# Gates of the second plain pair ahead of the first token-major group in a macaron trunk

## The chip, the cores and the metric

The kernel runs on one core of a Trainium2 chip. The metric is device time in microseconds (us) of one execution, the median of several runs. The profile is of one execution of its own.

## The reference

Two layers. Each has a feed-forward block (FFN), a mixing block of three attentions, and a second FFN, with a norm on both sides of every block. In the kernel the FFNs are named a0, c0, a1, c1, and the mixing blocks b0, b1. Only the FFN is touched by the change:

```python
def _swiglu(t, w_gate, w_up, w_down):
    return (jax.nn.silu(t @ w_gate) * (t @ w_up)) @ w_down
...
    f = _swiglu(_rmsnorm(h, ffn1_pre_g[l]), ffn1_w_gate[l], ffn1_w_up[l], ffn1_w_down[l])
    h = h + 0.5 * _rmsnorm(f, ffn1_post_g[l])
```

There are 512 tokens, a model width of 1024 and 2816 hidden features, 22 blocks of 128. All is float32.

## The kernel before

**Precision.** Every operand of a large product is split into a high part (ScalarE, L188) and a low part (VectorE, source minus high part, L189). A product is three matmuls (L214 to L216): high by high, high by low, low by high. So each unit of weights (128 x 1024 elements, 512 KB) passes through a landing buffer ("raw", 2 buffers) and then through one buffer each of "wh" and "wl" (4 of each). A unit's buffers come free when the matmuls that read it are done. The transfers are issued by SyncE (SP) in order.

**An FFN** works through its 22 feature blocks in three ways.

1. *The halved pair*, blocks 16 and 17, is computed first, one half of the tokens after the other, with features on the partitions. It holds four PSUM banks of the tag "mm" (two gates, two ups; there are four of that tag). `hidden` then forms silu(gate) x up and splits it.
2. *The token-major groups*, blocks 0 to 15 in four groups of four, are computed by a seven-product scheme over halves of tokens, columns and the inner dimension. Its products are numbered 0 to 6, and each takes 24 matmuls of 512 columns and two units of weights. Products 0, 1 and 6 read the inputs themselves (tiles us), products 2 to 5 read sums of inputs (tiles ag), which `sums` prepares in three steps on VectorE and ScalarE. Products 2, 3, 5 and 6 also form sums of weights on VectorE (L337, L340, L345, L349). The first group runs in the order 0 to 6: product 0 and product 1 open two "mm" banks each, product 3 accumulates on those of product 0, and product 2 opens another two, so that it needs those of product 1 back, which VectorE has added into the result by then (L749). The other groups run in the order 0, 2, 3, 4, 5, 1, 6. At the end of a group `feature_major` turns the result.
3. *The plain pairs*, blocks 18, 19 and 20, 21, are computed feature-major over all tokens: `gates` makes two banks of 48 matmuls in all, `ups` two more, and `hidden` combines them.

**The down projection** of blocks 0 to 15 is the same scheme with seven products for each of two halves (`downs(0)`, `downs(1)`; tiles pd, on four banks "z"). For each product VectorE also prepares the other factor (`first_factor`, L849 to L855) and adds the result (L889). The plain pairs stand between these products. Blocks 16 to 21 follow in a plain down projection.

**Order.** `ffn` puts jobs in a queue Q, each with its weight units. When a job starts, the units of the next jobs are loaded ahead, four at most (`load_ahead`), and their transfers are started as far as the landing buffers allow (`fetch_ahead`). Within that the framework orders the instructions of each engine by its own estimate. In program order the jobs around the change are: both halves of the halved pair (with step 1 of the sums in the second half), `park` (saves the residual to HBM), step 2 of the sums, product 0 of the first group, step 3, products 1 to 6, the other groups, down products 0 and 2, the gates of 18 and 19, the last group's turn, down products 3, 4, 5, the ups of 18 and 19, down products 1 and 6, then 0, 2, 3 of the second half, the gates of 20 and 21, 4, 5, 1, 6, the ups of 20 and 21. Between gates and ups the two gate banks stay occupied. Temporary tiles (`tmp`) have the tag f32t with 5 buffers.

Of the kernel before, what the change touches and what calls it, by code (L numbers as in the profile page):

```python
# [17 lines left out]
P = 128  # L18
# [4 lines left out]
def kernel(  # L23
# [39 lines left out]
    _, S, D = x.shape  # L63
# [3 lines left out]
    ND = D // P  # L67
# [32 lines left out]
    def tmp(name):  # L100
        return sb.tile([P, S], F32, tag="f32t", bufs=5, name=name)
# [6 lines left out]
    def blk(tag, name):  # L108
        return stile([P, 2, S], tag, name)

    def pbank(tag, name):
        return ps.tile([P, S], F32, tag=tag, bufs=4, name=name)
# [72 lines left out]
    def split(h_ap, l_ap, src, scale=None, later=False):  # L185

        if scale is None:
            both = [nc.scalar.copy(h_ap, src)]  # L188
            make = lambda: nc.vector.tensor_tensor(l_ap, src, h_ap.bitcast(F32), ALU.subtract)  # L189
        else:  # L190
            both = [nc.scalar.activation(h_ap, src, AF.Copy, scale=scale)]
            make = lambda: nc.vector.scalar_tensor_tensor(l_ap, src, scale, h_ap.bitcast(F32), ALU.mult, ALU.subtract)
        if later:
            return make
        both.append(make())
        if Q.pinned:
            for ins in both:
                tc.keep_in_program_order(ins)
# [13 lines left out]
    def mm3(pt, lh, ll, rh, rl, start, stop, free=False):  # L212

        nc.tensor.matmul(pt, lh, rh, start=start, stop=False, skip_group_check=free)  # L214
        nc.tensor.matmul(pt, lh, rl, start=False, stop=False, skip_group_check=free)  # L215
        nc.tensor.matmul(pt, ll, rh, start=False, stop=stop, skip_group_check=free)  # L216

    def gemm(pt, units, m, act, ks=None):

        last = sum(un.nk for un in units) - 1  # L220
        for un in units:
            for k in range(un.nk):
                kk = un.k0 + k
                if ks is not None and kk not in ks:
                    continue
                c = slice(m * P, (m + 1) * P)
                ah, al = act(kk)
                mm3(pt, un.h[:, k, c], un.l[:, k, c], ah, al, kk == 0, kk == last)
                yield 3 * pt.shape[1] * PE_US
# [138 lines left out]
    def wpair(src, ktiles, c0, name, scale=None):  # L368

        return [Unit(src, k, min(4, ktiles - k), c0, 256, f"{name}_{k}", scale) for k in range(0, ktiles, 4)]  # L370
# [110 lines left out]
    Q = Queue()  # L481
# [162 lines left out]
    def ffn(l, src, wg, wu, wd, dst, name, spare, aside=None):  # L644
# [5 lines left out]
        hid, st = {}, {}  # L650
        hr = {}
        act = lambda k, c=FULL: quad_act(src.us)(k, c)

        def hidden(f, pg, pu):
            s = tmp(f"s{name}_{f}")
            nc.scalar.activation(s[:], pg[:], AF.Silu)
            nc.vector.tensor_tensor(s[:], pu[:], s[:], ALU.mult)
            t = blk("q" if f < EARLY + 2 else "o", f"hid{name}_{f}")
            hid[f] = t[:, 0], t[:, 1]
            split(*hid[f], s[:])  # L660
            if f == NF - 1:
                tc.keep_in_program_order(nc.scalar.preload_act_table_set("natural_log_exp_and_others"))
# [124 lines left out]
        def park():  # L787

            if src.name != "x":
                for t in range(NT):  # L790
                    nc.sync.dma_start(hsave[t], hT[t][:])

        def halved(f, ug, uu, half):
            if half == 0:
                st["p"] = [pbank("mm", f"p{x}{name}_{f + m}") for x in "gu" for m in range(2)]
            else:
                Q.hold, Q.pinned = False, True
                Q.load_ahead()
                Q.pinned = False
                next(summed)  # L800
            c = HALVES[half]

            for uns, pts in ((ug, st["p"][:2]), (uu, st["p"][2:])):
                for low in (False, True):
                    for un in uns:
                        for k, (m, pt) in itertools.product(range(un.nk), enumerate(pts)):
                            kk, cols = un.k0 + k, slice(m * P, (m + 1) * P)
                            wh, wl = un.h[:, k, cols], un.l[:, k, cols]
                            ah, al = act(kk, c)
                            if low:  # L810
                                nc.tensor.matmul(pt[:, c], wh, al, start=False, stop=False, skip_group_check=True)
                                nc.tensor.matmul(pt[:, c], wl, ah, start=False, stop=kk == ND - 1, skip_group_check=True)
                            else:
                                nc.tensor.matmul(pt[:, c], wh, ah, start=kk == 0, stop=False, skip_group_check=True)
                            yield (1 + low) * S // 2 * PE_US
            if half == 1:
                for m in range(2):
                    hidden(f + m, st["p"][m], st["p"][2 + m])

        def gates(f, ug):  # L820
            st[f] = [pbank("mm", f"pg{name}_{f + m}") for m in range(2)]
            for m in range(2):
                yield from gemm(st[f][m][:], ug, m, act)

        def ups(f, uu):
            for m in range(2):
                pu = pbank("mm", f"pu{name}_{f + m}")
                yield from gemm(pu[:], uu, m, act)
                hidden(f + m, st[f][m], pu)
# [78 lines left out]
        def behind():  # L908
            for job in later:
                Q.add(*job)  # L910
            later.clear()

        def some(n):
            for one in itertools.islice(todo, n):
                Q.add(*one)

        def turns(f):
            *jobs, turn = group(f)
            later.append(turn)
            return iter(jobs)  # L920

        def downs(ci):
            Q.add([], lambda: iter(first_factor(ci, 0) or ()))
            return products(ci)

        ug, uu = (wpair(w[l], ND, EARLY * P, f"{x}{name}_{EARLY}") for x, w in (("g", wg), ("u", wu)))
# [4 lines left out]
        add_sums = lambda: Q.add([], lambda: iter(next(summed) or ()))  # L931
        Q.add(ug + uu, lambda: halved(EARLY, ug, uu, 0), src.ready((0, 1)))
        Q.add([], lambda: halved(EARLY, ug, uu, 1), src.ready(range(NT)))
        Q.add([], lambda: iter(park() or ()))
        marks["first"] = len(Q.jobs)
        add_sums()
        todo = turns(TG[0])
        some(1)
        add_sums()
        some(7)  # L940
        if name == "a0":
            Q.add([], vectors)
            Q.add([], lambda: iter(mem_stats() or ()))
        for g in TG[1:]:
# [3 lines left out]
            behind()  # L948
            some(7)
            later[:] = over  # L950
        pairs = [(wpair(wg[l], ND, f * P, f"g{name}_{f}"), wpair(wu[l], ND, f * P, f"u{name}_{f}")) for f in (18, 20)]
        todo = downs(0)
        some(2)
        Q.add(pairs[0][0], lambda: gates(18, pairs[0][0]))
        behind()
        some(3)
        Q.add(pairs[0][1], lambda: ups(18, pairs[0][1]))
        some(7)
        todo = downs(1)
        some(3)  # L960
        norm = aside() if aside is not None else None
        Q.add(pairs[1][0], lambda: gates(20, pairs[1][0]))
        some(4)
        if aside is not None:
# [753 lines left out]
    for l in LAYERS:  # L1718
        i, mn = 3 * l, []
        ma = ffn(l, subs[i], ffn1_w_gate, ffn1_w_up, ffn1_w_down, subs[i + 1], f"a{l}", "v",  # L1720
                 lambda l=l, mn=mn: mem_norm(l, mn))
        values = mem_kv(l, mn, *kvs[l])
        mb = mixing(l, subs[i + 1], *kvs[l], values, subs[i + 2])
        if l == 0:
            Q.weave(begin(), ma["first"])
            more_constants()
        else:
            for part, units in zip(mc["next"], (ma["early"][:2], ma["early"][2:])):
                part.extend(units)
            boundary(mc, mc["end"], ma["first"])  # L1730
        boundary(ma, ma["end"], mb["first"])
        mb["run"]()
        mc = ffn(l, subs[i + 2], ffn2_w_gate, ffn2_w_up, ffn2_w_down, subs[i + 3], f"c{l}", "o")
        for part, units in zip(mb["next"], (mc["early"][:2], mc["early"][2:])):
                part.extend(units)
        boundary(mb, mb["end"], mc["first"])
# [25 lines left out]
```

## Time and profile before

| | |
|---|---|
| median of 3 runs | 2427.16 us (2426.83 to 2427.58) |
| profiled execution, time | 2428.36 us |
| profiled execution, span | 2426.6 us |
| mean granted TensorE clock | 0.99 |
| TensorE busy | 2380.1 us, 98% of the span |
| VectorE busy | 1872.7 us, 77% |
| ScalarE busy | 1402.5 us, 58% |
| HBM traffic | 143 GB/s over the span |

Rows of the profile name the engine (PE, PEld, DVE, ACT, POOL, SP), the line of the kernel, and the tiles as output<-inputs with their numbers left out. A letter at the end of a tile's name is the FFN's (pta and ptc are banks of token-major products in a0 and a1, and in c0 and c1; pda and pdc are those of the down products; pga and pgc are gates). In brackets stands the time that the engine sat idle just before, and who ended it. Matmuls overlap: the step from one start to the next is the pace, and the duration is longer than that.

### The profile page before, as it was taken

How to read it: one execution, taken by the hardware profiler on the slowest of the kernel's cores; microseconds unless marked ns; L12 is line 12 of the kernel's file. 1: busy time of each engine (PE TensorE's matmuls, PEld its weight loads, DVE VectorE, ACT ScalarE, POOL GpSimd, SP SyncE). 2: the span in 40 equal slices, each digit the busy share in tenths (PEclk: the TensorE clock that was granted, in tenths of full speed). 3: DMA queues.
4: the chain of work that ended last, by engine and by line, in shares of the span. 5: the costliest groups of instructions: out<-in, count | busy, mean ns of one | idle time of the engine just before them, and what ended most of it. 6: DMA issues, size and time to landing. Idle time of an engine off the chain costs nothing.

```text
span 2426.6 us, 31086 instructions
## 1 busy us (share of the span) xinstructions
PE 2380.1 (98%) x11688; PEld 2003.4 (83%) x11688; DVE 1872.7 (77%) x2532; ACT 1402.5 (58%) x2291; POOL 74.1 (3%) x130
## 2 busy tenths in 40 slices
PE   8999999999999999999989999999999999899998
PEld 6788888888888887888878888888888888788887
DVE  8788877678777687788787888676787866788885
ACT  5656555577665554565645664556675655556654
POOL 1000000001010000000000000000001100000000
PEclk9999999999999999999999999999999999999999
DMA  5465475222223454644635555642232244455544
GB/s 174 156 209 156 156 241 159 72 80 75 82 68 121 148 165 131 216 149 154 220 129 183 179 159 175 232 131 79 62 88 79 77 132 140 138 177 179 165 165 165
DMA packets 232603, 349.73 MB, mean 144 GB/s; under 512 B 10730, under 2 KB 117506, under 8 KB 231940
## 3 DMA queue, kind: packets, MB, share of 16 engines
q1 hardware_dynamic: 232352, 347.71, 45.2%
q8 instruction: 92, 1.51, 0.3%
q14 instruction: 59, 0.48, 0.1%
q0 software_dynamic: 96, 0.03, 0.0%
q10 hardware_dynamic: 4, 0.00, 0.0%
HBM read 333.02 MB, written 14.68 MB: 143 GB/s over the span
## 4 chain that ended last, share of the span: by engine, by line
PE 81%; DVE 8%; DMA 4%; ACT 3%; issue 2%; POOL 0%; DVEq 0%; ACTq 0%; POOLq 0%
PE pg L216 3%; PE pg L214 3%; PE pg L215 3%; PE ptc L215 3%; PE ptc L216 3%; PE pta L215 3%; PE ptc L214 3%; PE pta L216 3%; PE pta L214 3%; PE pdc L214 2%; PE pdc L215 2%; PE pdc L216 2%; PE pda L215 2%; PE pda L214 2%; PE pda L216 2%
## 5 line engine op out<-in xcount | busy, mean ns | idle before, releaser
L214 PE MATMUL pg<-us_a,wh_wg 128*128 128x512 f32 x384 | 151.0, 393 | 0.0
L216 PE MATMUL pg<-us_a,wl_wg 128*128 128x512 f32 x384 | 149.7, 390 | 0.0
L215 PE MATMUL pg<-us_a,wh_wg 128*128 128x512 f32 x384 | 149.6, 390 | 0.0
L188 ACT CAST wh_ta<-kta 128x1024 fp32r<-128x1024 f32 x80 | 83.3, 1053 | 92.2 <-DVE kta L337 26.2
L188 ACT CAST wh_tc<-ktc 128x1024 fp32r<-128x1024 f32 x80 | 83.2, 1051 | 88.1 <-DVE ktc L337 24.4
L189 DVE TENSOR_TENSOR wl_tc<-ktc,wh_tc 128x1024 fp32r<-128x1024 f32 x80 | 96.8, 1222 | 35.9 <-ACT wh_tc L188 35.5
L189 DVE TENSOR_TENSOR wl_ta<-kta,wh_ta 128x1024 fp32r<-128x1024 f32 x80 | 96.9, 1222 | 33.6 <-ACT wh_ta L188 33.3
L214 PE MATMUL pta<-wh_ta,aga 128*128 128x512 f32 x256 | 102.9, 404 | 13.6 <-ACT wh_ta L188 11.7
L214 PE MATMUL ptc<-wh_tc,agc 128*128 128x512 f32 x256 | 102.4, 401 | 9.8 <-ACT wh_tc L188 9.8
L215 PE MATMUL ptc<-wl_tc,agc 128*128 128x512 f32 x256 | 102.2, 399 | 3.5 <-DVE wl_tc L189 3.5
L215 PE MATMUL pta<-wl_ta,aga 128*128 128x512 f32 x256 | 102.6, 401 | 3.0 <-DVE wl_ta L189 3.0
L216 PE MATMUL pta<-wh_ta,aga 128*128 128x512 f32 x256 | 101.9, 398 | 0.0
L216 PE MATMUL ptc<-wh_tc,agc 128*128 128x512 f32 x256 | 101.6, 397 | 0.0
L214 PE MATMUL pda<-wh_da,aha 128*128 128x512 f32 x224 | 87.3, 390 | 0.0
L214 PE MATMUL pdc<-wh_dc,ahc 128*128 128x512 f32 x224 | 87.3, 390 | 0.0
L215 PE MATMUL pda<-wl_da,aha 128*128 128x512 f32 x224 | 87.2, 389 | 0.0
L215 PE MATMUL pdc<-wl_dc,ahc 128*128 128x512 f32 x224 | 87.1, 389 | 0.0
L216 PE MATMUL pdc<-wh_dc,alc 128*128 128x512 f32 x224 | 86.8, 389 | 0.0
L216 PE MATMUL pda<-wh_da,ala 128*128 128x512 f32 x224 | 86.8, 389 | 0.0
L216 PEld LDWEIGHTS pg<-us_a,wl_wg 128*128 128x128 f32 x384 | 72.1, 188 | 15.3
L215 PEld LDWEIGHTS pg<-us_a,wh_wg 128*128 128x128 f32 x384 | 72.2, 188 | 14.1
L214 PEld LDWEIGHTS pg<-us_a,wh_wg 128*128 128x128 f32 x384 | 72.1, 188 | 14.1
(543 smaller groups left out, 7522.3 us busy)
## 6 DMA issues: line engine op xcount, KB each, us to landing
raw_ta<-in_ffn_w_gate_dram SPq DMA_DIRECT2D x64, 512.0 KB, 3.8
raw_tc<-in_ffn_w_gate_dram SPq DMA_DIRECT2D x64, 512.0 KB, 3.8
raw_da<-in_ffn_w_down_dram SPq DMA_DIRECT2D x58, 512.0 KB, 3.9
raw_dc<-in_ffn_w_down_dram SPq DMA_DIRECT2D x58, 512.0 KB, 3.5
raw_wg<-in_w_gate_dram SPq DMA_DIRECT2D x48, 512.0 KB, 3.6
kta<-in_ffn_w_up_dram SPq DMA_DIRECT2D x32, 512.0 KB, 5.6
ktc<-in_ffn_w_up_dram SPq DMA_DIRECT2D x32, 512.0 KB, 5.8
raw_wo<-in_w_out_dram SPq DMA_DIRECT2D x24, 512.0 KB, 3.4
```

What stands on the lines that cost most here:

```text
L188: both = [nc.scalar.copy(h_ap, src)]
L189: make = lambda: nc.vector.tensor_tensor(l_ap, src, h_ap.bitcast(F32), ALU.subtract)
L214: nc.tensor.matmul(pt, lh, rh, start=start, stop=False, skip_group_check=free)
L215: nc.tensor.matmul(pt, lh, rl, start=False, stop=False, skip_group_check=free)
L216: nc.tensor.matmul(pt, ll, rh, start=False, stop=stop, skip_group_check=free)
```

## The change

The gates of blocks 18 and 19 are queued behind step 2 of the sums and ahead of the first token-major group, with step 3 of the sums behind them. Each of the two gate banks is passed through silu as soon as its matmuls are done; the result stays in SBUF until the ups of 18 and 19, and the banks come free. In the down projection the gates are gone from their place behind product 2, and the ups of 18 and 19 are queued behind product 3 in place of product 5.

```diff
@@ ffn @@
-        def hidden(f, pg, pu):
+        def silu(f, pg):
             s = tmp(f"s{name}_{f}")
             nc.scalar.activation(s[:], pg[:], AF.Silu)
+            return s
+
+        def hidden(f, pg, pu):
+            s = silu(f, pg) if pg is not None else st.pop(("silu", f))
             nc.vector.tensor_tensor(s[:], pu[:], s[:], ALU.mult)
...
-        def gates(f, ug):
+        def gates(f, ug, ahead=False):
             st[f] = [pbank("mm", f"pg{name}_{f + m}") for m in range(2)]
             for m in range(2):
                 yield from gemm(st[f][m][:], ug, m, act)
+                if ahead:
+                    st["silu", f + m], st[f][m] = silu(f + m, st[f][m]), None
...
         marks["first"] = len(Q.jobs)
+        pairs = [(wpair(wg[l], ND, f * P, f"g{name}_{f}"), wpair(wu[l], ND, f * P, f"u{name}_{f}")) for f in (18, 20)]
+        add_sums()
+        Q.add(pairs[0][0], lambda: gates(18, pairs[0][0], True))
         add_sums()
         todo = turns(TG[0])
-        some(1)
-        add_sums()
-        some(7)
+        some(8)
...
-        pairs = [(wpair(wg[l], ND, f * P, f"g{name}_{f}"), wpair(wu[l], ND, f * P, f"u{name}_{f}")) for f in (18, 20)]
         todo = downs(0)
         some(2)
-        Q.add(pairs[0][0], lambda: gates(18, pairs[0][0]))
         behind()
-        some(3)
+        some(1)
         Q.add(pairs[0][1], lambda: ups(18, pairs[0][1]))
         some(7)
```

## The prediction

> **What bounds the kernel now.** I read the page first, for who is busy.
>
> ```profile
> span 2426.6 us, 31086 instructions
> ...
> PE 2380.1 (98%) x11688; PEld 2003.4 (83%) x11688; DVE 1872.7 (77%) x2532; ACT 1402.5 (58%) x2291; POOL 74.1 (3%) x130
> ```
>
> TensorE (PE) is the bound, so only its stops and its slow stretches can be won. The second view is the list of who waited for whom, PE alone, over the whole span (us in total, times, longest).
>
> ```profile
> PE pta L214 <- ACT wh_ta L188: 11.7, 2, 6.7
> PE ptc L214 <- ACT wh_tc L188: 9.8, 2, 4.9
> PE ptc L215 <- DVE wl_tc L189: 3.5, 3, 1.5
> PE pta L215 <- DVE wl_ta L189: 3.0, 2, 1.5
> ...
> PE ptc L214 <- ACT sc L656: 1.0, 2, 0.8
> ```
>
> Two waits in the a-layers and two in the c-layers: one per feed-forward block (FFN), four in all. They belong to pta/ptc, the banks of the token-major groups. The third view is PE's timeline around the one of the first c-layer (start and duration in us).
>
> ```profile
> 893.37 0.40 PE L214 MATMUL ptc<-wh_tc,us_b 128*128 128x512 f32 x1
> ...
> 905.20 0.39 PE L216 MATMUL ptc<-wh_tc,us_b 128*128 128x512 f32 x1
> 910.49 1.22 PE L214 MATMUL ptc<-wh_tc,agc 128*128 128x512 f32 x2 [4.90 <-ACT wh_tc L188]
> 913.20 0.80 PE L215 MATMUL ptc<-wl_tc,agc 128*128 128x512 f32 x1 [1.49 <-DVE wl_tc L189]
> ...
> 914.22 0.63 PE L215 MATMUL ptc<-wl_tc,agc 128*128 128x512 f32 x1
> 914.64 0.63 PE L216 MATMUL ptc<-wh_tc,agc 128*128 128x512 f32 x1
> ...
> 918.75 0.39 PE L214 MATMUL ptc<-wh_tc,agc 128*128 128x512 f32 x1
> ```
>
> Products 0 and 1 of group 0 (inputs us_b) run from 893.37 to 905.43, then the first product on the summed inputs (agc) waits. After the wait the step between starts is 0.43 us (914.22 to 914.64) until 918.75, from where a matmul lasts 0.39 again as it did before. The windows of this stretch show the clock and who works meanwhile (length, then PE, PEld, DVE, ACT, POOL busy and counts, granted PE clock, DMA share, GB/s).
>
> ```profile
> 905.43:910.49 5.06, 0.16 (x2) 0.01 (x1) 5.06 (x5) 2.99 (x4) 0.00 (x0) 0.78 0.18 68
> 910.49:918.75 8.26, 6.77 (x15) 4.86 (x16) 4.98 (x6) 1.95 (x2) 0.00 (x0) 0.51 0.00 0
> ```
>
> VectorE (DVE) is busy for all 5.06 us in which PE stands: the bound here is DVE. Its own timeline says with what.
>
> ```profile
> 893.62 1.23 DVE L189 TENSOR_TENSOR wl_tc<-raw_tc,wh_tc 128x1024 fp32r<-128x1024 f32 x1 [1.38 <-ACT wh_tc L188]
> ...
> 900.57 2.35 DVE L337 TENSOR_TENSOR ktc<-ktc,raw_tc 128x1024 f32<-128x1024 f32 x2
> 902.84 1.22 DVE L677 TENSOR_TENSOR rc<-us_b 128x1024 f32<-128x1024 f32 x1
> ...
> 911.92 2.35 DVE L189 TENSOR_TENSOR wl_tc<-ktc,wh_tc 128x1024 fp32r<-128x1024 f32 x2
> 914.19 1.28 DVE L749 TENSOR_TENSOR cc<-cc,ptc 128x512 f32<-128x512 f32 x2
> 921.47 1.23 DVE L189 TENSOR_TENSOR wl_tc<-ktc,wh_tc 128x1024 fp32r<-128x1024 f32 x1 [6.00 <-ACT wh_tc L188]
> ```
>
> From 893.62 to 915.47 DVE never rests: the end of the halved pair, input sums (L677), and the weights of products 1 (L189 at 893.62), 2 (L337 at 900.57) and 3 (L189 at 911.92). Then it rests for 6.00 us: a backlog of one moment, no lasting shortage. The end of it is what PE wants twice over. Product 3's low weights come at 911.92. And product 1 is added into its result (L749) at 914.19, before which product 2 has no PSUM: there are four "mm" banks, products 0 and 1 hold two each, and product 0's pair is kept for product 3. So PE starts on product 3 and gets no further.
>
> **What one stop costs.** In the last window PE issues 15 matmuls, 15 x 0.227 = 3.40 us at full pace. From 905.43 to 918.75 are 13.32 us, so 9.92 us are lost: 4.90 + 1.49 idle, and 3.53 in the slow clock. Over the four FFNs, with the same 3.53 for each: 11.7 + 9.8 for the first waits, 4 x 1.5 for the second, 4 x 3.53 for the clock = 41.6, and 1.0 for the bank that waits for the halved pair's silu (L656): 42.6 us, 10.65 per FFN. That is all that can be won here.
>
> On the clock the Trainium skill ("TensorE: Matmul & The Clock Gate", Part 1) says that the array falls to half its rate after an idle window of about 3.4 us and needs about 3.4 us of work to come back. The step of 0.43 us against 0.227, behind 4.90 us of idleness, agrees. By that rule a wait that stays under 3.4 us would cost its own length alone.
>
> **The change, part by part.** The gates of blocks 18 and 19 are 2 x 8 x 3 = 48 matmuls. Where they stand now, the windows show what they take, and the whole stretch from the first down product to the gates of 20 (here in the last FFN, columns as above):
>
> ```profile
> 2275.35:2286.24 10.89, 10.89 (x50) 8.96 (x49) 9.37 (x11) 5.71 (x8) 0.00 (x0) 1.00 0.32 109
> ...
> 2264.47:2337.42 72.95, 72.73 (x329) 60.24 (x328) 60.94 (x68) 42.64 (x59) 0.00 (x0) 1.00 0.53 171
> ```
>
> 10.89 / 48 = 0.227 us is the full pace used above. They cost PE 10.89 us in either place: nothing is won by them themselves.
>
> *New place.* PE runs gates from 893.4 to 904.3, product 0 to 909.7, product 1 to 915.2 (5.44 us each, 24 matmuls). Weights are loaded in the order of the queue: the gates' two units take the place that product 0's had, so they are there at 893.4; product 0's take that of product 1's, ready at about 894.9, needed at 904.3. DVE's backlog grows by the two low parts of product 1's units, 2.27 us (900.57 to 902.84 is the step of two such). It therefore reaches product 1's addition (914.19 before) at 916.5, and PE comes to it at 915.2 where it came at 905.43. What is left: 916.5 + 1.28 - 915.2 = 2.6 us, of which product 3's first unit (12 matmuls, 2.7 us) covers all if its weights are there: lower bound zero. The upper bound comes from the casts,
>
> ```profile
> L188 ACT CAST wh_tc<-ktc 128x1024 fp32r<-128x1024 f32 x80 | 83.2, 1051 | 88.1 <-DVE ktc L337 24.4
> ```
>
> as the second unit of product 3 can be cast only once product 1 has released its weight buffer at 915.2; with cast 1.05, low part 1.23 and addition 1.28 in front of PE that is 3.6 us, and with the clock falling again (3.53) 7.1. I take 1.5, nearer the lower end, because DVE's six idle microseconds show that nothing else stands behind the backlog.
>
> *Silu kept.* Two activations move from the ups to the gates, no more of them and no table load, since the halved pair's silu comes just ahead. Their two tiles hold 2 of the 5 buffers of f32t until the ups; nothing in the token-major groups asks for that tag. Zero. On ScalarE's queue the silu of 18 waits for its eight k-steps, with casts queued behind; those casts wait for the same matmuls to release weight buffers. Zero, else in the 1.5.
>
> *Queues.* The two loads of the gates move ahead of those of product 0 on SP.
>
> ```profile
> raw_tc<-in_ffn_w_gate_dram SPq DMA_DIRECT2D x64, 512.0 KB, 3.8
> ...
> raw_gc<-in_ffn_w_gate_dram SPq DMA_DIRECT2D x12, 512.0 KB, 4.2
> ```
>
> 0.4 us longer to land than a product's, with 10.89 us of new matmuls to hide in: zero. The four stores of h (park) wait behind them and nobody waits for those.
>
> *Old place.* Gates were cover there: 10.89 us of PE against 2.27 of their own DVE work. Without them the stretch is 62.06 us of PE, and DVE has 60.94 - 2.3 = 58.6 to do: it fits, with 3.4 to spare, where 12.0 were. What DVE waits for in that stretch is in the waits (its two largest rows of seven):
>
> ```profile
> DVE wl_dc L189 <- ACT wh_dc L188: 6.8, 8, 1.6
> DVE sc L657 <- PE puc L216: 1.4, 2, 0.8
> ```
>
> and for PE in the same stretch, to the end of the interleaved product behind it:
>
> ```profile
> PE pgc L216 <- DVE wl_gc L189: 0.4, 1, 0.4
> ```
>
> I read the first kind as casts held back until PE releases a buffer: there DVE is ahead and could use the time. The last row is the gates of 20, at 2338: there PE has no slack left even now. The ups also move forward by two products, so the uncovered run behind them is 4, 5, 1, 6 and then 0, 2, 3 of the second half, instead of 1, 6, 0, 2, 3. Products 4 and 5 carry for DVE: the low parts of hidden 18 and 19 1.28, factors for 5 and 1 2.56 + 1.28, weights for 1 and 6 2.27 + 4.54, additions of 4 1.28 (1.28 for two 512-wide operations, as at 914.19): 13.2 us against 10.9 of PE, 2.3 us late at a point without slack. Bounds: 0, as 3.4 us are spare in the sum; 8.0, if the 11.4 us that DVE waits in this stretch (the sum of the seven rows) all stayed, 70.0 against 62.06. I take 2.
>
> **Sum.** 42.6 - 4 x 1.5 - 4 x 2 = 28.6 us. The profiled execution took 2428.36 us (span 2426.6); the median of the three timed runs is 1.20 lower, 2427.16. So 2427.16 - 28.6 = 2398.6 us, 1.2% faster. With nothing given back 2384.6; with 3.6 and 4 per FFN 2415.
>
> **Rivals.** *All is won* (0.12): additions ahead of weights in DVE's queue, and PE's order fills the downs; 2385. For it: PE had no idle there but 0.4 us.
>
> *The start stops again* (0.06): product 2's bank comes late by 3.6 and the clock falls: 42.6 - 4 x 7.1 - 8 = 6.2 won, 2421. For it: DVE executes in order and the addition stood behind product 3's weights. Against: 9 us more to work in. By the window that the Trainium skill gives (the page named above) a wait of 3.6 us lies at the edge. Without the fall of the clock the same rival gives 2407.
>
> *DVE becomes the bound of the downs* (0.05): 8 us there, 42.6 - 6 - 32 = 4.6 won, 2422.6, no change that can be told. Against: 58.6 in 62.06.
>
> *Slower* (0.06): the stop only changes its place, and is longer there. Without cover DVE falls behind in the seven products in a row, PE stands 8 us before the gates of 20, and the clock falls as it did behind 905 (3.53), so 11.5 per FFN; and the start keeps 1.5. 42.6 - 6 - 46 = 9.4 lost, 2437. It decides from a loss of 9.2 us per FFN in the downs on. Against it: short waits between products, each under 2 us, leave the clock alone.
>
> *It doesn't do what it says* (0.03): the framework orders each engine's instructions itself and could run product 0 before the gates; then PE meets the same backlog with gates as filler, or not at all: 2427. Against it: gates come earlier in the program and their weights are first.
>
> **How the numbers follow.** The forecast has 0.68. Below 2385 lies nothing that I can name; from 2385 to 2414 lie the forecast and all-is-won, 0.80, and the range is that. A difference under 0.2% (4.9 us) can't be told from none. Faster by more than that: forecast, all-is-won, start-stops-again, 0.86; within: DVE-bound downs and no-effect, 0.08; slower 0.06.
>
> **What the profile after would show.** Right: between the halved pair and the first agc matmul 48 matmuls on pga/pgc; the waits of pta/ptc for wh and wl down from 21.5 and 6.5 us to under 8 together; no 0.43 us steps in group 0; the window of 62 us from the first down product to gates 20 longer by 1 to 3 us; waits of pd matmuls or gates 20 for wl of 1 to 2 us each FFN. Wrong: a wait of over 3.4 us left at product 2 or new in the downs, with the granted clock under 1.00 behind it.

## The result and the profile after

The change takes 2400.72 us (median of 4 runs, 2395.15 to 2405.31) against 2427.26 us: a ratio of 0.989, 95% interval 0.9868 to 0.9912, so 26.5 us faster. The forecast was 2398.6, with 2385 to 2414. Two later sessions gave 0.9882 (0.9868 to 0.9895) and 0.9888 (0.9868 to 0.9908). The profiled execution took 2399.02 us; its page says:

```profile
span 2397.3 us, 31090 instructions
...
PE 2369.5 (99%) x11688; PEld 1996.4 (83%) x11688; DVE 1870.9 (78%) x2532; ACT 1399.4 (58%) x2291; POOL 73.9 (3%) x130
```

VectorE does what it did (1872.7 us before). PE's busy time fell by 10.6 us with the same matmuls: those that ran at half clock behind the four stops don't any more. One phase of half clock is left, 3.41 us from 111.5 us on, in the first a-layer; the kernel before has it too, from 109.6 us on. PE's waits over the span, the largest:

```profile
PE ptc L214 <- ACT wh_tc L188: 3.1, 2, 2.2
PE ptc L215 <- DVE wl_tc L189: 2.8, 3, 1.5
PE pta L215 <- DVE wl_ta L189: 2.4, 3, 1.0
PE pta L214 <- ACT wh_ta L188: 2.3, 2, 1.5
PE pta L214 <- ACT ca L751: 2.2, 2, 1.2
```

The four rows on wh and wl were 28.0 us and are 10.6, where the prediction gave under 8 as a sign of being right; two later profiles have 9.4 and 15.8. The first c-layer on PE's timeline, where before there was the stop of 905 to 913:

```profile
886.78 0.40 PE L214 MATMUL pgc<-us_b,wh_gc 128*128 128x512 f32 x1
...
897.69 0.39 PE L214 MATMUL ptc<-wh_tc,us_b 128*128 128x512 f32 x1
...
908.35 0.39 PE L216 MATMUL ptc<-wh_tc,us_b 128*128 128x512 f32 x1
910.96 1.15 PE L214 MATMUL ptc<-wh_tc,agc 128*128 128x512 f32 x3 [2.23 <-ACT wh_tc L188]
911.94 0.39 PE L215 MATMUL ptc<-wl_tc,agc 128*128 128x512 f32 x1
```

Gates from 886.78, products 0 and 1 from 897.69, and 2.23 us of idleness are left, without the slow clock behind them (0.39 us at once). In the downs, from the first down product to the gates of 20 in the last FFN, there is this window, and what VectorE waits for in it:

```profile
2246.31:2308.86 62.55, 62.55 (x286) 51.99 (x285) 58.23 (x66) 39.91 (x57) 0.00 (x0) 1.00 0.54 178
```

```profile
DVE wl_dc L189 <- ACT wh_dc L188: 1.5, 2, 1.0
DVE alc L189 <- ACT ahc L188: 1.2, 1, 1.2
DVE btc L337 <- DMA raw_dc<-in_ffn_w_down_dram: 1.1, 2, 0.6
```

VectorE is busy for 58.23 of 62.55 us, and its wait for wh_dc fell from 6.8 us to 1.5. That wait was mostly slack: the stretch takes 0.5 us more than the 62.06 of the sum on paper (the prediction looked for 1 to 3), and at the gates of 20 PE waits 0.5 us where it waited 0.4:

```profile
PE pgc L216 <- DVE wl_gc L189: 0.5, 1, 0.5
```

For the comparisons below I read three stretches of each profile off the starts of PE's rows and summed them over the four FFNs: A, from the halved pair's last matmul to the first on summed inputs (gates or spare matmuls included); B, from there to the first down product; C, from there to the last product of `downs(1)`, up to its last matmul but one. The last column takes out the work that a kernel has more or less than before in A and C (4 x 10.89 = 43.56 us), so its differences are losses.

| profile | A | B | C | A, C at the work before |
|---|---|---|---|---|
| before | 68.3 | 612.6 | 446.3 | 68.3, 446.3 |
| the change | 93.7 | 600.3 | 405.0 | 50.1, 448.6 |
| the change, second profile | 93.1 | 598.4 | 403.1 | 49.5, 446.7 |
| the change, third profile | 97.5 | 608.0 | 406.0 | 54.0, 449.5 |
| silu kept, gates in the old place | 67.7 | 611.0 | 445.8 | 67.7, 445.8 |
| spare matmuls in the new place | 87.6 | 597.6 | 447.9 | 44.1, 447.9 |
| spare matmuls in the old place | 94.8 | 601.1 | 447.6 | 51.3, 447.6 |
| ups kept late | 92.3 | 597.0 | 406.9 | 48.8, 450.5 |
| sums without additions | 46.7 | 595.5 | 446.2 | 46.7, 446.2 |
| gates behind product 0 | 89.8 | 595.6 | 404.5 | 46.2, 448.1 |
| the same, second profile | 90.3 | 598.2 | 405.4 | 46.8, 449.0 |

At full pace A is 48 matmuls in each of four FFNs, 43.5 to 44 us: the kernel before lost some 24 there, the change loses 6 to 10. (The row with silu kept comes from a later session and does the work of the kernel before in its order, but for the two silu: its differences from the first row, 0.6, 1.6 and 0.5, show the spread to keep in mind.)

### The profile page after: what moved, and what is told of

Read it like the earlier page. It is cut to its first block, busy times and chain, and to the rows that moved or that the text cites. A ratio compares the mean times of both kernels' runs of the same rounds, so it can differ in the third digit from the quotient of the medians.

```text
span 2397.3 us, 31090 instructions
## 1 busy us (share of the span) xinstructions
PE 2369.5 (99%) x11688; PEld 1996.4 (83%) x11688; DVE 1870.9 (78%) x2532; ACT 1399.4 (58%) x2291; POOL 73.9 (3%) x130
## 4 chain that ended last, share of the span: by engine, by line
PE 80%; DVE 8%; DMA 6%; ACT 3%; issue 2%; SPq 0%; DVEq 0%; ACTq 0%
PE pg L214 3%; PE pg L216 3%; PE pg L215 3%; PE ptc L215 3%; PE ptc L214 3%; PE ptc L216 3%; PE pta L214 3%; PE pta L215 3%; PE pta L216 3%; PE pdc L216 2%; PE pdc L215 2%; PE pdc L214 2%; PE pb L214 2%; PE pb L215 2%; PE pb L216 2%
## 5 line engine op out<-in xcount | busy, mean ns | idle before, releaser
L215 PE MATMUL pda<-wl_da,aha 128*128 128x512 f32 x224 | 87.6, 391 | 0.8 <-DVE wl_da L189 0.8
L215 PEld LDWEIGHTS pg<-us_a,wh_wg 128*128 128x128 f32 x384 | 72.2, 188 | 14.1
L214 PEld LDWEIGHTS pg<-us_a,wh_wg 128*128 128x128 f32 x384 | 72.1, 188 | 14.1
```

## The experiments

Kernels of one session share the runs of the kernel before, whose median went from 2423.71 to 2427.58 us between the sessions. So ratios are compared.

**VectorE's work ahead of product 2 (sums without additions).** The eight additions of `whole` and `block_sum` are left out of the kernel before:

```diff
 def whole(i, j):
-    t = st["r", i, j] = stile([P, 4, S // 2], "f", f"r{name}_{i}{j}", F32)
-    nc.vector.tensor_tensor(t[:], <high part>, <low part>, ALU.add)
+    st["r", i, j] = src.us[j][:, :, 0, HALVES[i]].bitcast(F32)
 def block_sum(n, to, a, b, op, tag):
-    r = st["r", to // 10, to % 10][:]
-    nc.vector.tensor_tensor(r, *(st["r", x // 10, x % 10][:] for x in (a, b)), op)
-    st["a", n] = r, tag
+    st["a", n] = st["r", to // 10, to % 10], tag
```

> The kernel before, with the eight 128x1024 additions and subtractions of the input sums left out on VectorE (products 2 to 5 read a high part of the inputs in place of a sum); casts, low parts, transfers and matmuls stay. VectorE has 8 x 1.13 = 9 us less to do ahead of product 2 in each FFN. Theory (VectorE's backlog holds product 2 up): the stop of 10.6 us per FFN goes down to 1 to 3, 31 to 38 us faster than before. Rival (weight transfers and their two landing buffers hold it up, VectorE only waits along): the weights of product 3 come no sooner, less than 8 us faster.

Ratio 0.9855 (0.9842 to 0.9868), 36 us faster; the waits for wh are gone from its list:

```profile
PE pta L215 <- DVE wl_ta L189: 2.1, 3, 1.1
PE pta L214 <- DVE ca L745: 2.1, 1, 2.1
PE ptc L215 <- DVE wl_tc L189: 1.6, 2, 1.1
```

Transfers, casts and matmuls were the same, and PE had waited there for weights (wh_tc), not for the sums themselves; so the stop before was VectorE's backlog. VectorE's busy time fell by 33.0 us (1872.7 to 1839.7), A and B together by 38.7 us.

**The new place alone (spare matmuls there).** The kernel before with

```diff
+def filler():
+    pt = pbank("z", f"spare{name}")
+    for k in range(48):
+        ah = src.us[k % 2][:, k % 4, 0, :]
+        nc.tensor.matmul(pt[:], ah[:, 0:P], ah, start=k == 0, stop=k == 47, skip_group_check=True)
+        yield S * PE_US
...
 add_sums()
+Q.add([], filler)
 todo = turns(TG[0])
```

> The kernel before, with 48 spare matmuls of 512 columns, whose result nobody reads, in the place where the change puts the gates; the gates stay behind down product 2. So the new place alone, with cover and without the loss of cover in the downs, and without more weights to prepare. Theory (TensorE stood there because VectorE had a backlog, 42.6 us at most over four FFNs): the spare work costs 4 x 10.89 = 43.6 and takes 33 to 42 out, so 2428 to 2438. Rival (the stop is tied to something that starts when product 0 starts, so it moves along): 2427 + 43.6 = 2471.

Ratio 1.0033 (1.0021 to 1.0045), 7.5 us slower: 43.56 us of work went in, 36.1 us of stop came out. Its rows, the spare matmuls in the first c-layer and the only wait left there:

```profile
L835 PE MATMUL sparec<-us_b 128*128 128x512 f32 x48 | 11.1, 390 | 0.0
```

```profile
919.54 0.50 PE L215 MATMUL ptc<-wl_tc,agc 128*128 128x512 f32 x1 [1.29 <-DVE wl_tc L189]
```

So cover is what the place gives: 36.1 of the 42.6 us can be had there by cover that needs no weights.

**The old place alone (spare matmuls there, in the changed kernel).** The same `filler`, on a "mm" bank, queued behind down product 2.

```diff
 some(2)
+Q.add([], filler)
 behind()
 some(1)
```

> The change, with 48 spare matmuls of 512 columns, read by nobody, in the place in the down projection from which the gates were taken. They cost 4 x 10.89 = 43.6 us and give the cover back. Theory of the prediction (2 us per FFN lost there): 43.6 - 8 = 36 us slower than the change. Rival (the changed profile shows 2 to 4 us more of waits there than before, over all FFNs): 40 to 43 us slower.

Ratio 1.0054 (1.0042 to 1.0066) against 0.9882 for the change one session earlier: 0.0172, or 41.7 us, where 43.56 of work went in. The cover gave back 1.9 us, with the two intervals leaving -3 to 6. In the table C is 447.6, as in kernels whose downs have their old order (445.8 to 447.9), where the change has 446.7 to 449.5. So the loss of cover cost about 2 us in all; the 8 of the theory lie outside the interval.

**The change once more.** It ran again in a session with three of the other kernels.

> The changed kernel once more, for its spread and a second profile. Theory (the stop in front of product 2 is gone and what is left there hangs on when two weight transfers land): about 2400 us, single runs again some us apart, 2395 to 2406, where the kernel before stays within 1 us; the remaining waits of pta/ptc move between the FFNs from one profile to the other. Rival (the spread of the first four runs was an accident of that session): all runs within 1 us of one value between 2398 and 2402.

Ratio 0.9882 (0.9868 to 0.9895): 2394.59 us (4 runs, 2392.91 to 2395.91) against 2423.71 us. The kernel before went from 2421.92 to 2428.21 us over its 16 runs of that session, so it spreads by 6 us itself, against the 1 us that was expected, and the changed kernel's runs lie within 3 us: a spread alone tells nothing here. What does vary from one profile of the change to the next is the wait at product 2:

```profile
PE pta L214 <- ACT wh_ta L188: 2.8, 2, 1.9
PE ptc L214 <- ACT wh_tc L188: 2.0, 2, 1.0
```

In the first profile the c-layers had 2.2 us at the longest and the a-layers 1.5; here it is 1.0 and 1.9.

**The ups moved forward.** The change with `some(3)` in place of `some(1)` ahead of the ups of 18.

> The change, but the ups of 18 and 19 stay behind down product 5, where they were; the gates alone move. Theory of the prediction (the two products that lost their place ahead of the ups make VectorE late at the gates of 20, about 2 us per FFN): 2393 to 2397, faster than the change by 3 to 8 us. Rival 1 (the changed profile shows only some 2 us more wait at the gates of 20 over all four FFNs, so the place of the ups hardly matters): within 2 us of the change. Rival 2 (five products in a row without the gates as cover: 0, 2, 3, 4, 5): waits of 2 to 4 us per FFN ahead of the ups, 2408 to 2416.

0.9898 (0.9885 to 0.9912) against 0.9882 (0.9868 to 0.9895) in the same session, 2398.32 to 2394.59 us: if anything slower, though the intervals overlap. Its profile has waits that the change has not, in the downs:

```profile
PE pda L216 <- DVE ala L189: 1.9, 2, 0.9
PE pdc L216 <- DVE alc L189: 1.9, 2, 1.0
```

Five products without cover make the low part of a factor late, by 1 us in each FFN. The theory that moving the ups costs 2 us per FFN fell, and rival 2's sizes did too; rival 1's "within 2 us" can't be told apart from the 3.7 measured.

**Silu kept in SBUF, gates in their old place.** In the kernel before, `gates(18, ...)` calls silu on each bank, as in the change.

> The kernel before, with the silu of 18 and 19 taken right behind their gates and kept in SBUF, the gates in their old place: that part of the change alone. Theory: nothing, 2426 to 2428. Rival (two PSUM banks that come free earlier help the turn and the ups): 2421 to 2425.

Ratio 0.9997 (0.9988 to 1.0006). It neither costs nor brings anything that can be told.

**What is left at product 2.** The changed profile shows it: VectorE's timeline in the first c-layer.

```profile
898.83 2.35 DVE L189 TENSOR_TENSOR wl_tc<-raw_tc,wh_tc 128x1024 fp32r<-128x1024 f32 x2
903.91 1.23 DVE L337 TENSOR_TENSOR ktc<-ktc,raw_tc 128x1024 f32<-128x1024 f32 x1 [2.72 <-DMA raw_tc<-in_ffn_w_gate_dram]
...
908.53 1.22 DVE L340 TENSOR_TENSOR ktc<-ktc,ktc 128x1024 f32<-128x1024 f32 x1
909.73 1.22 DVE L189 TENSOR_TENSOR wl_tc<-ktc,wh_tc 128x1024 fp32r<-128x1024 f32 x1
910.87 0.68 DVE L753 TENSOR_TENSOR cc<-cc,ptc 128x512 f32<-128x512 f32 x1
```

VectorE now rests for 2.72 us where it had its backlog: product 1's units (898.83) hold the landing buffers, and the transfer for product 2 (L337) starts behind them; product 3's (L340), on which PE starts here as before, comes behind that. The bound has gone from VectorE to the landing buffers. What kept product 1's units there differs. In a1 and c1 the second of them was cast just when the gates' last matmuls gave up a weight buffer (1241.66 and 2084.44), and PE's waits at product 2 were 0.75 and 0.90 us. In a0 and c0, with 1.53 and 2.23 us, ScalarE's queue came on top:

```profile
895.47 2.00 ACT L188 CAST agc<-rc 128x1024 fp32r<-128x1024 f32 x2 [0.20 <-DVE rc L687]
897.37 2.00 ACT L188 CAST wh_tc<-raw_tc 128x1024 fp32r<-128x1024 f32 x2
```

In c0 the high part of the gates' first unit was read for the last time until 894.9, but the casts of the input sums stood ahead in ScalarE's order. To test the landing buffers as the bound, the gates were queued one job later, behind product 0, so that product 1's units take product 0's buffers early:

```diff
-Q.add(pairs[0][0], lambda: gates(18, pairs[0][0], True))
-add_sums()
 todo = turns(TG[0])
-some(8)
+some(1)
+Q.add(pairs[0][0], lambda: gates(18, pairs[0][0], True))
+add_sums()
+some(7)
```

> The change with the gates one job later: behind product 0 of the first group, ahead of product 1. Theory for what is left at product 2 (in the changed profile product 1's two units can't be cast until the gates release their weight buffers, so they hold both landing buffers and product 2's transfers start late): product 1's units now take the buffers of product 0, early, and the wait of 1.2 to 2.7 us per FFN at product 2 goes; 3 to 7 us faster than the change, 2388 to 2392 where that has 2395. Back comes the wait of product 0 for the bank of silu 17, 1 us in all. Rival (what is left is product 1's addition on VectorE and the bank that it frees): as before it, within 2 us of the change.

Ratio 0.9855 (0.9842 to 0.9868), 2389.64 us: the fastest version. Here the same VectorE rows come during the gates:

```profile
892.77 1.22 DVE L189 TENSOR_TENSOR wl_tc<-raw_tc,wh_tc 128x1024 fp32r<-128x1024 f32 x1
...
895.49 1.23 DVE L337 TENSOR_TENSOR ktc<-ktc,raw_tc 128x1024 f32<-128x1024 f32 x1 [0.36 <-DMA raw_tc<-in_ffn_w_gate_dram]
```

and PE goes from product 1 into the summed inputs without a rest, and pays for it with the wait for silu 17's bank in product 0:

```profile
886.15 0.50 PE L214 MATMUL ptc<-wh_tc,us_b 128*128 128x512 f32 x1 [1.01 <-ACT sc L656]
...
907.33 0.39 PE L216 MATMUL ptc<-wh_tc,us_b 128*128 128x512 f32 x1
907.55 0.39 PE L214 MATMUL ptc<-wh_tc,agc 128*128 128x512 f32 x1
```

VectorE has the same work in both, so what remained in the change was not the amount of it. The run moves product 1's casts ahead of both hindrances at once, the gates' weight buffers and the casts of the input sums; how much each of them cost is not shown. With the ups late on top of it:

> Gates behind product 0, and the ups behind down product 5 as before the change. If the place of the ups costs nothing either way (the ups kept late alone: ratio 0.9898 against 0.9882), within 3 us of the gates-behind-product-0 kernel; if the ups are better early by what those ratios say, 3 to 4 us slower than it.

0.9868 (0.9856 to 0.9881), 2392.27 us, 2.6 us slower than with the ups early; the intervals overlap.

**Both on one chip.**

> The change beside the kernel with the gates behind product 0, on one chip, as their ratios so far (0.9882 and 0.9855) came from two sessions. Theory (landing buffers held by product 1's units make product 2's transfers late, and those of product 6 after them): ratio 0.988 to 0.989, and the waits of 1 to 2.4 us at product 2 and about 0.9 us at product 6 in the c-layers and a1 are there again. Rival (the gap was the sessions'): both kernels within 2 us.

> The gates behind product 0 once more. Theory: 0.985 to 0.986, 4 to 8 us faster than the change beside it, no wait over 0.5 us at product 2. Rival: within 2 us of the change.

The change 0.9888 (0.9868 to 0.9908), 2401.56 us; gates behind product 0 0.9863 (0.9844 to 0.9882), 2393.44 us. The medians are 8 us apart, the intervals overlap; the order is that of the earlier sessions. The theory's "no wait over 0.5 us" holds in three FFNs; the first a-layer keeps one of 1.43 us. The profiled execution of the change was a long one this time (2411.54 us), and shows one thing that can lengthen a run:

```profile
911.90 1.23 DVE L340 TENSOR_TENSOR ktc<-ktc,ktc 128x1024 f32<-128x1024 f32 x1 [0.88 <-DMA ktc<-in_ffn_w_up_dram]
```

```profile
914.33 1.65 PE L214 MATMUL ptc<-wh_tc,agc 128*128 128x512 f32 x3 [3.60 <-ACT wh_tc L188]
915.78 0.63 PE L215 MATMUL ptc<-wl_tc,agc 128*128 128x512 f32 x1
```

The transfer for product 3 landed later (7.7 us after its issue, 6.6 in the first profile), VectorE waited for it, PE stood for 3.60 us, and the clock fell. That is the size that the prediction gave to the rival "the start stops again" (3.6 us and the clock), and the sign that it named for being wrong, in one FFN of one execution. It is not that rival's mechanism: PE waited for weights, not for product 2's bank. The clock also fell at the start of a0 and a1 in this execution.

## Why the prediction was right

The forecast of 28.6 us less met 26.5, and 29.1 and 26.0 in the later sessions. The mechanism is right; that the number fits so well is in part luck, as the steps show:

- **The bound.** Right. Leaving out eight additions per FFN on VectorE brought 36 us, and spare matmuls alone took 36.1 of the 42.6 us out.
- **What is left at the start**, 4 x 1.5. Right in size: the waits at the first product on summed inputs are 5.4 us in all (the two rows on wh) and 4.8 in the second profile, 9.3 in the long execution. The mechanism was half right. The upper bound was built on the weight buffer that a unit must wait for, and that is where the chain begins; but the likely value was put down to the length of VectorE's queue, and VectorE has rests there now. The landing buffers, named nowhere in that step, are what the wait hangs on.
- **The slow clock**, 14.1 us, all to go, and with it the second waits, 4 x 1.5. Both lie in B, 20 us together, and too much was expected: B fell by 12.3 and 14.2, in the long execution, with half clock behind three of the four starts, by 4.6. In the first profile new waits at product 6 (0.6 to 0.7 us per FFN) and in later groups (1.0 and 1.5 us) take most of the difference; the prediction had no term for them.
- **The old place**, 4 x 2. Mis-sized. C, at equal work, is 2.3, 0.4 and 3.2 us longer than before, where downs in their old order vary by 2.1 (445.8 to 447.9); the spare matmuls there gave back 1.9. The step that failed is "no slack at the gates of 20": the two products that went in front of it are late by the sum on paper, but VectorE's 11.4 us of waits in that stretch were mostly slack, and it used them (6.8 to 1.5 us for wh_dc). Over the four FFNs PE's waits for wl at the gates went from 1.9 to 2.5 us. The prediction had read VectorE's waits so and then didn't count them.
- **The ups.** The cost of moving them forward had the wrong sign: left behind product 5 they make PE wait about 1 us per FFN for the factors (3.8 us in all, and 3.5 with the gates behind product 0). The times, 3.7 and 2.6 us slower, point the same way within overlapping intervals.
- **The sum.** In the first profile A and B gave 30.5 us at equal work where 36.6 were forecast, and C cost 2.3 where 8 were. The two misses, 6.1 and 5.7 us, cancel; nothing in the prediction made them do so.
- **Zero terms.** Silu kept: 0.9997. The longer landing of the gates' transfers: no wait at their first matmul (886.78, 0.40).

On the clock, the Trainium skill ("TensorE: Matmul & The Clock Gate", Part 1) has an idle window of about 3.4 us, free-running. The free run agrees with these profiles, as the last section shows; that the window must be idle does not. In the kernel before, the clock fell at 908.29, 2.7 us after PE's last matmul had ended, and in the long execution 2.5 us after. So the reading in the prediction, that a shorter wait costs its own length alone, does not hold in these runs, nor does its "short waits between products, each under 2 us, leave the clock alone".

## What to carry to other kernels

Where the busiest engine stops once per stage while a helper works through a burst of preparation, ready work of the same length put into that place is worth the stop and the slow clock behind it; spare work there prices it before anything is moved. Count what the moved work holds while it runs: here two weight buffers, through which the bound went to the landing buffers of the next loads, and putting it one job later gave some 6 us more by the ratios of two sessions, whose intervals touch or overlap. Where it is taken from, look at what the helper waits for: its waits for buffers to come free were mostly slack here, and a deficit on paper is to be set against them first.

## What the runs showed of the hardware that was not expected

A short wait sometimes drops the clock. In two executions of the kernel with the gates behind product 0, PE waited 1.43 us in the first a-layer. In one nothing followed:

```profile
62.34 0.50 PE L215 MATMUL pta<-wl_ta,aga 128*128 128x512 f32 x1 [1.43 <-DVE wl_ta L189]
```

```profile
63.70:67.10 3.40, 3.40 (x17) 2.82 (x16) 0.91 (x2) 1.60 (x2) 0.00 (x0) 1.00 0.02 5
```

In the other the granted clock was halved for 3.4 us, 1.3 us after PE had started again:

```profile
63.26 0.50 PE L215 MATMUL pta<-wl_ta,aga 128*128 128x512 f32 x1 [1.43 <-DVE wl_ta L189]
```

```profile
64.60:68.00 3.40, 3.40 (x10) 2.63 (x9) 0.94 (x2) 1.06 (x1) 0.00 (x0) 0.50 0.02 5
```

10 matmuls in place of 17: about 1.6 us. In the long execution of the change waits of 1.72 and 2.55 us were followed by it too, while in the first profile 2.23 us were not. The kernel before has a case already: waits of 0.89 and 1.03 us in the first a-layer.

```profile
106.16:109.57 3.41, 1.72 (x6) 1.15 (x7) 1.25 (x2) 3.38 (x7) 0.00 (x0) 1.00 0.00 0
109.57:112.98 3.41, 3.41 (x9) 2.65 (x9) 1.88 (x6) 3.41 (x7) 0.00 (x0) 0.50 0.55 154
```

No run was made to find what decides it, but the clock records of the twelve profiles largely tell. All half-clock phases of an execution begin on one grid of 3.413 us (within 4 ns), wherever the waits lie. Cut into the windows of that grid, from 10 to 2330 us and at full clock, the profiles have 20 windows in which PE was busy for 53.2% of the time or less: half clock followed all 20. It followed none of some 8090 in which PE was busy for 59.5% or more, and 1 of the 10 in between. So a wait counts by what it takes out of one window: the 2.23 us lie across a boundary and leave 1.93 and 2.67 us busy,

```profile
906.80:910.21 3.41, 1.93 (x9) 1.28 (x7) 3.41 (x4) 1.39 (x2) 0.00 (x0) 1.00 1.05 359
910.21:913.63 3.42, 2.67 (x11) 1.98 (x12) 3.42 (x4) 0.69 (x1) 0.00 (x0) 1.00 0.41 149
```

and the two waits of 1.43 us lie each within one, at the edge, with 2.00 us busy where nothing followed and 1.98 where the clock fell:

```profile
60.92:64.33 3.41, 2.00 (x9) 1.66 (x10) 3.41 (x5) 1.22 (x3) 0.00 (x0) 1.00 0.02 5
61.21:64.62 3.41, 1.98 (x10) 1.40 (x9) 3.41 (x4) 1.22 (x3) 0.00 (x0) 1.00 0.07 28
```

What decides between 53.2% and 59.5% stays open.
